# A hybrid decoder step on one core: where norms, decay rows, inverses and loads stand at three borders between stages

## The chip, the core and the metric

The kernel is one program on one core of a Trainium2 chip. The metric is device time in microseconds (us), median over runs; lower is better. TensorE (PE) multiplies matrices, VectorE (DVE), ScalarE (ACT) and GpSimd (POOL) work on tiles, and every transfer is issued by SyncE (SP). Each engine executes its own instructions strictly in the order in which the program wrote them and waits on semaphores for the others.

## The reference, cut to what matters

One inference step of a two-layer decoder: layer 0 mixes tokens with a gated DeltaNet, layer 1 with causal pooling, and each layer ends in a gated ConvFFN. There are 1024 prompt tokens with 16 meta tokens ahead, and 64 sample tokens (8 sequences of 8): 1104 columns, worked on as three chunks of 368. All arithmetic is in 32-bit floats.

```python
h = rmsnorm(x, w)                                    # norm of the layer's input
proj = h @ w_in                                      # q, k, v (8 heads each), z (8), b and a (one narrow item)
qkv = silu(causal_dwconv(conv_state, qkv, conv_w))   # width 4; last 3 columns are an output (gconv)
q, k = l2norm(q) * DK**-0.5, l2norm(k)
g = -exp(A_log) * softplus(a + dt_bias); G = cumsum(g)
decay = exp(G_i - G_j)                               # i >= j
T = inverse(I + strict_lower(beta * (k @ k.T) * decay))   # per chunk of 64
U, W = T @ (v*beta), T @ (k*beta*exp(G)); A = (q @ k.T) * decay
# recurrence over chunks:  v_new = U - W S;  o = (q exp(G)) S + A v_new;  S = S exp(G_end) + k_dec.T v_new
x = x + (rmsnorm(o) * silu(z)) @ w_out
x = x + ConvFFN(rmsnorm(x))                          # up, width-3 conv, gate, down
```

## The kernel before

**Matmuls.** Activations lie transposed, 128 features by columns. A matmul in full precision is made of three with split operands: a tile is rounded into a high part (whi, hhi, ghi: a cast on ACT) and a low part (wlo, hlo, glo: the difference, on POOL or DVE), and PE does hi·hi (line 279), lo·hi (280) and hi·lo (281). A weight tile of 128x512 comes by DMA into wst; `Stream.fetch` issues that load and `Stream.prep` writes the two instructions that split it (lines 162 and 163).

**What sets the order.** Python generators write the program. A generator yields a cost, and a small scheduler (`Slots`: a count of ticks and a heap) resumes it when that many ticks have gone by; the main loop ticks as it writes its matmuls. So the order within each engine's row is fixed when the program is written. `Job` chains a generator behind another; `delayed(n, gen)` starts one n ticks later. In the recurrence `weave` mixes the chain of one head with fillers (the next head's preparation, the output projection wo): each filler is due in proportion between two shares of the chain, such as 0.0 to 0.88.

**Start.** `rstd_steps` squares a chunk on ACT (nsq), adds the squares on DVE (nac, line 307) and sums over features on PE (ss, line 311); `scale_steps` then multiplies by the root (nhf, line 333) and splits (hhi on ACT, hlo on DVE or POOL by `even` and `odd`, lines 336 and 339). Chunk 0's norm is written first. `a_first(c)` writes the first four projection items of chunk c, 96 matmuls, while chunk c+1 is normed; chunk 1's sum is paced by `upto`, chunk 2's by `delayed`.

**Projections.** 33 items, in the order of a table, each 3 chunks of 24 matmuls. `conv_chunk` does the width-4 convolution of a q, k or v item (ACT, line 394, then three steps on DVE, line 402; in the last chunk also raw, tailp and three short steps on line 407). A z item has no convolution, a silu alone. Beside them `rows_steps` makes the decay rows (a scan of g on DVE, then R by subtractions), `k_steps` each head's k·k and the matrix Q, and `inverses` all heads' triangular inverses as one long row of DVE pairs (tb and X, lines 562 and 564). At its end X is stored (xb), copied transposed into Qb (line 597) and stored (xt).

**Recurrence.** `load(h)` issues a head's loads (lG, lq, lk, lE, lv), `load2(h)` those of its inverse (lQ, Tbd and Xbd from xt and xb, l8). `newton(h)` corrects the inverse on PE (nw). `prep(h)` makes qk and its decayed form AT, transposes, and so on; `chain(h)` runs the state through the chunks (pc, op). `nxt(0)`, woven into head 0's chain, writes load(1), the loads of xT (the residual, three times 1472 KB), and the first weights of wo (`wd.fetch`, wst from w_out).

**First ConvFFN.** While the last wo matmuls run, chunks of xT are finished (line 1235) and normed (`norm_steps`), and the up-projection's weights are fetched and split (`wu.prep`, `wu.fetch`).

Of the kernel before, what the change touches and what calls it, by code (L numbers as in the profile page):

```python
# [12 lines left out]
AF = mybir.ActivationFunctionType  # L13
ALU = mybir.AluOpType
# [27 lines left out]
TAIL0 = 1024  # L42
# [171 lines left out]
def build(nc, tc, I, O, stop=None):  # L214
    es = ExitStack()
    V, A, G, T, SY = nc.vector, nc.scalar, nc.gpsimd, nc.tensor, nc.sync
    slots = Slots()
# [40 lines left out]
    def v3(a, t=P):  # L258
        return a.rearrange("p (u t) -> p u t", t=t)
# [57 lines left out]
        out.append(r)  # L317
        yield pace

    def norm_steps(xc, wcol, c, tp, psp, tag, pace=1, pace2=1):  # L320
        out = []
        yield from rstd_steps(xc, tp, psp, tag, out, pace)
        yield from scale_steps(xc, wcol, c, tp, out[0], pace=pace2)

    def scale_steps(xc, wcol, c, tp, r, even=V, odd=G, pace=1):
        s = hcol(c, 0, CH)
# [45 lines left out]
    order = [("ba", 0), ("k", 0), ("k", 1), ("k", 2), ("v", 0), ("v", 1), ("v", 2)]  # L372
    order += [("k", h) for h in range(3, H)]

    order += [(t[0], int(t[1])) for t in "q0 q1 z0 q2 z1 q3 z2 q4 z3 q5 z4 q6 z5 q7 z6 v3 z7 v4 v5 v6 v7".split()]
    base = {"q": 0, "k": 8, "v": 16, "z": 24}
    tid = [32 if kd == "ba" else base[kd] + h for kd, h in order]

# [70 lines left out]
    def rows_steps(lg):  # L449
        a_ = slice(32, 40)  # L450
        R = kp.tile([P, NTP], F32, tag="Q", name="R", bufs=2)
        sm = kp.tile([P, NTP], F32, tag="E", name="sm", bufs=2)
        g = kp.tile([P, NTP], F32, tag="E", name="g", bufs=2)
        t1 = kp.tile([P, NTP], F32, tag="Gb", name="t1", bufs=2)[:, :NT]
        t2 = kp.tile([P, NTP], F32, tag="Bb", name="t2", bufs=2)[:, :NT]
        nA = ab.tile([P, 1], F32, name="nA")
        SY.dma_start(out=sm, in_=I["scanm"])
        G.memset(R, 0.0)
        G.memset(g[a_], 0.0)
        silu(R[0:8, :NT], lg[0:8, :NT], AF.Sigmoid)  # L460
        yield 2
        A.activation(t1[a_], lg[a_, :NT], AF.Abs, bias=cv[a_, C_DTB:C_DTB + 1])
        A.activation(t2[a_], lg[a_, :NT], AF.Relu, bias=cv[a_, C_DTB:C_DTB + 1])
        lnexp()
        A.activation(nA[a_], cv[a_, C_ALOG:C_ALOG + 1], AF.Exp)
        yield 1
        A.activation(t1[a_], t1[a_], AF.Exp, scale=-1.0)
        yield 1
        A.activation(t1[a_], t1[a_], AF.Ln, bias=onec[a_])
        yield 2  # L470
        V.tensor_scalar(nA[a_], nA[a_], -1.0, None, op0=ALU.mult)
        V.tensor_tensor(t1[a_], t1[a_], t2[a_], op=ALU.add)
        V.tensor_scalar(g[a_, :NT], t1[a_], nA[a_], None, op0=ALU.mult)
        V.tensor_tensor_scan(R[a_], sm[a_], g[a_], 0.0, op0=ALU.mult, op1=ALU.add)
        SY.dma_start(out=brow_d, in_=R[0:8])
        SY.dma_start(out=grow_d, in_=R[a_])
        l_ = slice(64, 72)
        Gm = v3(R[a_, 0:TAIL0])
        V.tensor_tensor(v3(R[l_, 0:TAIL0]), Gm[:, :, P - 1:P].to_broadcast([8, 8, P]), Gm, op=ALU.subtract)
        Gp = R[a_, TAIL0:NPR]  # L480
        V.tensor_tensor(R[l_, TAIL0:NPR], Gp[:, N_META - 1:N_META].to_broadcast([8, N_META]),
                        Gp, op=ALU.subtract)
        Gs = v3(R[a_, NPR:NT], LS)
        V.tensor_tensor(v3(R[l_, NPR:NT], LS), Gs[:, :, LS - 1:LS].to_broadcast([8, NSEQ, LS]), Gs,
                        op=ALU.subtract)
        yield 16
# [80 lines left out]
    def inverses(sp):  # L567
        Qb = sp.tile([P, 64, 64], F32, name="Qb")
        Qt = sp.tile([P, 16, 16], F32, name="Qt")
        SY.dma_start(out=Qb, in_=qb_d)  # L570
        X = sp.tile([P, 64, 64], F32, name="X")
        tb = sp.tile([P, 1024], F32, name="tb")
        t8 = sp.tile([NTAIL, H * NTAIL], F32, name="t8")
        Xt = sp.tile([P, 16, 16], F32, name="Xt")
        G.memset(t8, 0.0)
        SY.dma_start(out=x8_d.rearrange("h p t -> p h t"), in_=v3(t8, NTAIL))
        for x, m in ((X, 64), (Xt, 16)):
            G.memset(x, 0.0)
# [12 lines left out]
        for a in range(nt):
            r = slice(16 * a, 16 * a + 16)
            SY.dma_start(out=x8_d[:, r, 16 * a:16 * a + 16], in_=Xt[8 * a:8 * a + 8])
        XT = Qb.rearrange("p b a -> p a b")
        SY.dma_start(out=xb_d, in_=flat(X))
        for r in range(0, 64, 16):
            A.copy(XT[:, r:r + 16, :], X[:, r:r + 16, :])
            yield 1.0
        SY.dma_start(out=xt_d, in_=flat(Qb))
        yield 1.0  # L600
# [72 lines left out]
    with ExitStack() as en:  # L673
# [5 lines left out]
        tp = TP()  # L679
# [51 lines left out]
        def delayed(n, gen):  # L731
            yield n
            yield from gen
# [21 lines left out]
        xload(2, 4)  # L755

        def upto(job, n, then):
            while not job.done:
                yield n
                job.step()  # L760
            yield from then

        third = slots.spawn(delayed(11, rstd(2, 1.4)))
        job = slots.spawn(upto(second, 1.6, scale(1, 0.25)))
        a_first(0)
        job.finish()
        job = slots.spawn(scale(2, 0.25), third)
# [131 lines left out]
    while bg:  # L899
        background(9.0)  # L900
    slots.drain()
    SY.dma_start(out=O["gconv_p"], in_=tailp)
    SY.dma_start(out=O["gconv_s"], in_=tails)
    if stop == "A":
        es_l.close()
        ea.close()
# [280 lines left out]
    r0 = []  # L1187
# [64 lines left out]
    def nxt(h):  # L1252
        if h == 0:
            yield from prep0
            load(1)
            for c in range(NCH):
                SY.dma_start(out=xT[:, :, ck_(c)], in_=I["xT"][c])
            wd.fetch()
            yield from newton(1, pq, "pq")
        if h + 1 < H:  # L1260
            yield from prep(h + 1)
            if h + 2 < H:
                load(h + 2)
            if h:
                while "Q" not in heads[h + 1]:
                    yield 0
                yield from newton(h + 1, pq, "pq")
            if h == 0:
                wd.need(1)
                wd.fetch()  # L1270
            nwj[h + 1] = True
# [4 lines left out]
        flush_pend()  # L1276
    chains = True
    zload(0, range(3))
    load2(1)
    banks = itertools.repeat((pw, "pw"))  # L1280

    def wbank():
# [3 lines left out]
    for h in range(H):  # L1286
        cur = nxt(h)
        if h == H - 1:
            early = later.spawn(early_norm())
        weave(chain(h), 24.0, [(cur, 7.45 if h else 10.35, 0.0, 0.88, True), (wo, 11.0 if h > 1 else 6.0, 0.0 if h > 1 else 0.45, 1.0, False)], flush_pend)  # L1290
    while later.q:
        later.tick()
        flush_pend()
# [28 lines left out]
    def xchunk(c):  # L1322
        return xT[:, :, ck_(c)]
# [303 lines left out]
    banks = itertools.cycle(((pw, "pw"), (pd, "pd")))  # L1627
    for _ in wo:
        slots.tick()
        wu.prep()  # L1630
        wu.fetch()

        while started < len(done):
            if started:
                gen = norm_steps(xchunk(started), C_NF0, started, ft, pd, "pd", 2.5, 2)
            else:
                gen = scale_steps(xchunk(0), C_NF0, 0, ft, r0[0], pace=2)
            jobs.append(slots.spawn(gen, jobs[-1] if jobs else None))
            started += 1
    now, begun = [0], set()  # L1640
# [167 lines left out]
```

## Time and profile before

| | |
|---|---|
| median of 3 runs | 2497.41 us (2495.71 to 2498.42) |
| profiled execution | 2497.63 us |
| its span, first to last instruction | 2495.9 us |
| mean granted TensorE clock | 0.986 |
| busy: PE, DVE, ACT, POOL | 2401.8, 1513.1, 969.5, 861.0 us |
| chain that ended last, share of PE, DVE, ACT, issue | 74%, 12%, 4%, 4% |
| DMA moved | 345.04 MB, mean 138 GB/s |

In rows of instructions the first number is the start in us from the span's beginning, the second the duration (of a merged row with xN: from the first's start to the last's end), then engine, line, operation, out<-in, and in brackets how long the engine stood idle before it and what it waited for. A row of the list of waits gives who waited for whom: us in total, times, longest.

### The profile page before, as it was taken

Reading aid. Unit: us, or ns where it says so; the run is one execution under the profiler, and the core shown is the slowest. Engines: PE = TensorE matmul, PEld = TensorE weight load, DVE = VectorE, ACT = ScalarE, POOL = GpSimd, SP = SyncE. Lnnn points to the kernel's source line nnn. Section 1 sums busy time; section 2 is a strip of 40 time slices with the busy share of each in tenths; the row PEclk is TensorE's granted clock in tenths of the full one; section 3 lists DMA queues with packets and bytes.
Section 4 is the critical chain, followed back from the end, with each engine's and each line's share of the span. In section 5 each row is a group of like instructions: output and inputs, shape, how many; then the busy total and the mean of one; then the engine's idle time right before and its main releaser. Section 6 shows DMA issues by size and latency. Waiting matters only on the chain.

```text
span 2495.9 us, 38634 instructions
## 1 busy us (share of the span) xinstructions
PE 2401.8 (96%) x14393; PEld 2347.4 (94%) x14393; DVE 1513.1 (61%) x3010; ACT 969.5 (39%) x2088; POOL 861.0 (34%) x967
## 2 busy tenths in 40 slices
PE   8999999879999799999999999999999999999997
PEld 6899998879998799999999999999999999999996
DVE  6576799535556745555555545787644555555556
ACT  5677222364553533333333213334323223222334
POOL 3366332133333544554554101211113323332342
PEclk9999999989999899999999999999999999999999
DMA  3366421595641235545444366577763111111112
GB/s 137 118 215 219 162 86 64 181 290 176 197 138 49 73 114 171 170 151 172 160 167 153 130 224 199 190 231 191 218 206 129 43 43 47 47 39 47 43 60 80
DMA packets 198684, 345.04 MB, mean 138 GB/s; under 512 B 55504, under 2 KB 66128, under 8 KB 198112
## 3 DMA queue, kind: packets, MB, share of 16 engines
q1 hardware_dynamic: 198496, 342.56, 41.7%
q8 instruction: 114, 1.87, 0.3%
q14 instruction: 74, 0.61, 0.1%
HBM read 258.88 MB, written 83.61 MB: 137 GB/s over the span
## 4 chain that ended last, share of the span: by engine, by line
PE 74%; DVE 12%; ACT 4%; issue 4%; POOL 2%; DMA 2%; SPq 1%; DVEq 0%; POOLq 0%; ACTq 0%
PE up L281 13%; PE up L279 13%; PE up L280 13%; PE dn L279 6%; PE dn L281 6%; PE dn L280 6%; DVE X L564 2%; DVE tb L562 2%; PE ps L279 2%; DVE acc L402 2%; PE ps L280 2%; PE ps L281 2%; PE pool L1497 1%; PE nw L839 1%; DVE acc L1373 1%
## 5 line engine op out<-in xcount | busy, mean ns | idle before, releaser
L279 PE MATMUL up<-hhi,whi 128*128 128x370 f32 (+2 forms) x2112 | 705.2, 334 | 0.0
L1373 DVE SCALAR_TENSOR_TENSOR acc<-up,cv,acc 128x368 f32<-128x368 f32 (+4 forms) x528 | 303.7, 575 | 657.0 <-ACT acc L1365 408.3
L281 PE MATMUL up<-hhi,wlo 128*128 128x370 f32 (+2 forms) x2112 | 698.9, 331 | 0.0
L280 PE MATMUL up<-hlo,whi 128*128 128x370 f32 (+2 forms) x2112 | 696.9, 330 | 0.2 <-POOL hlo L339 0.2
L163 POOL TENSOR_TENSOR wlo<-wst,whi 128x512 fp32r<-128x512 f32 x286 | 381.3, 1344 | 384.8 <-ACT whi L162 370.0
L1437 DVE TENSOR_TENSOR xT<-xT,dn 128x368 f32<-128x368 f32 (+1 forms) x864 | 408.8, 527 | 2.8 <-PE dn L281 2.7
L280 PEld LDWEIGHTS up<-hlo,whi 128*128 128x128 f32 x2112 | 399.1, 189 | 2.6 <-POOL hlo L339 0.5
L279 PEld LDWEIGHTS up<-hhi,whi 128*128 128x128 f32 x2112 | 397.6, 188 | 2.1 <-issue 0.3
L281 PEld LDWEIGHTS up<-hhi,wlo 128*128 128x128 f32 x2112 | 397.8, 188 | 0.0
L1365 ACT ACTIVATE acc<-up,cv 128x368 f32<-128x368 f32 (+1 forms) x264 | 173.2, 656 | 493.4 <-PE up L281 491.8
L279 PE MATMUL dn<-ghi,whi 128*128 128x368 f32 (+1 forms) x1056 | 349.0, 331 | 4.4 <-DVE xT L1437 2.9
L281 PE MATMUL dn<-ghi,wlo 128*128 128x368 f32 (+1 forms) x1056 | 346.1, 328 | 0.7 <-POOL wlo L163 0.7
L280 PE MATMUL dn<-glo,whi 128*128 128x368 f32 (+1 forms) x1056 | 346.0, 328 | 0.3 <-POOL glo L1411 0.3
L1411 POOL TENSOR_TENSOR glo<-acc,ghi 128x368 fp32r<-128x368 f32 (+1 forms) x132 | 133.2, 1009 | 596.7 <-ACT ghi L1410 572.9
L279 PE MATMUL ps<-hhi,whi 128*128 128x372 f32 (+1 forms) x792 | 269.2, 340 | 16.1 <-DVE acc L402 16.0
L280 PE MATMUL ps<-hlo,whi 128*128 128x372 f32 (+1 forms) x792 | 265.9, 336 | 0.9 <-DVE hlo L726 0.6
L281 PE MATMUL ps<-hhi,wlo 128*128 128x372 f32 (+1 forms) x792 | 265.0, 335 | 0.0
L162 ACT CAST whi<-wst 128x512 fp32r<-128x512 f32 x286 | 172.4, 617 | 89.9 <-PE up L280 43.3
L279 PEld LDWEIGHTS dn<-ghi,whi 128*128 128x128 f32 x1056 | 198.3, 188 | 6.6 <-DVE xT L1437 3.5
L280 PEld LDWEIGHTS dn<-glo,whi 128*128 128x128 f32 x1056 | 198.3, 188 | 1.8 <-POOL glo L1411 0.6
L281 PEld LDWEIGHTS dn<-ghi,wlo 128*128 128x128 f32 x1056 | 198.2, 188 | 1.1 <-POOL wlo L163 1.1
L1410 ACT CAST ghi<-acc 128x368 fp32r<-128x368 f32 (+1 forms) x132 | 65.8, 498 | 272.9 <-DVE acc L1408 272.9
(216 smaller groups left out, 3345.4 us busy)
## 6 DMA issues: line engine op xcount, KB each, us to landing
wst<-i_w_up SPq DMA_DIRECT2D x192, 256.0 KB
whi<-ws SPq DMA_DIRECT2D x128, 256.0 KB
wlo<-ws SPq DMA_DIRECT2D x128, 256.0 KB
wst<-i_w_dn SPq DMA_DIRECT2D x88, 256.0 KB
wst<-i_w_in SPq DMA_DIRECT2D x62, 256.0 KB
whi<-ws_None SPq DMA_DIRECT2D x56, 256.0 KB
wlo<-ws_None SPq DMA_DIRECT2D x56, 256.0 KB
ws<-whi SPq DMA_DIRECT2D x48, 256.0 KB
```

The costliest lines, as they stand in the source:

```text
L162: self.nc.scalar.copy(hi, st)
L163: self.nc.gpsimd.tensor_tensor(lo, st, hi.bitcast(F32), op=ALU.subtract)
L279: T.matmul(ps, hi[:, ws], rhi(k), start=start and j == 0, stop=False)
L280: T.matmul(ps, hi[:, ws], rlo(k), start=False, stop=False)
L281: T.matmul(ps, lo[:, ws], rhi(k), start=False, stop=stop and j == n - 1)
L402: V.scalar_tensor_tensor(acc[:, a:n], ps[:, o + a - d:o + n - d], w[3 - d], acc[:, a:n], op0=ALU.mult, op1=ALU.add)
L562: V.tensor_tensor(t, X[:n, 0:k, j:j + 1].to_broadcast([n, k, w]), Qb[:n, j:j + 1, j + 1:m].to_broadcast([n, k, w]), op=ALU.mult)
L1365: A.activation(acc[:, b:], ps[:, o + b:o + CH], AF.Identity, scale=w[2], bias=col(C_FCB + l * NUP + n))
L1373: V.scalar_tensor_tensor(acc[:, i:m], ps[:, o + i - d:o + m - d], w[2 - d], acc[:, i:m], op0=ALU.mult, op1=ALU.add)
L1410: A.copy(ghi, acc)
L1411: G.tensor_tensor(glo, acc, ghi.bitcast(F32), op=ALU.subtract)
L1437: V.tensor_tensor(xT[:, m, s], xT[:, m, s], ps[:, b:CH], op=ALU.add)
```

## The change

Ten edits:

1. Start: `upto` lets 10 ticks go by and then writes a step of the second norm each 0.5 ticks (before: a step each 1.6 from the start); the third norm starts after 15 ticks, not 11.
2. The table of items: z7 goes from between v3 and v4 to the end.
3. Decay rows: an add goes from DVE to POOL, the scaling by nA to ACT, three subtractions to POOL.
4. Inverses: the transposed copy goes from ACT, 4 of 128x1024, to POOL, 8 of 128x512.
5. gconv's two stores are issued when the last item has its first chunk, not after the last item.
6. `load2(1)` stands right behind the projections, ahead of zload(0).
7. In `nxt(0)`, w_out's first weights are fetched ahead of xT.
8. Head 1's preparation (h == 1 in `weave`) is due from a share of 0.2 of the chain, not 0.0; it makes head 2's.
9. First ConvFFN: weights are split and fetched only when chunk 0 is scaled; chunk 0 is scaled at a pace of 1.5 (2 before).
10. Its chunk 2 is normed at a pace of 3.8 (2.5 before) with all its splits on DVE.

```diff
@@ table of items
-    order += [(t[0], int(t[1])) for t in "q0 q1 z0 q2 z1 q3 z2 q4 z3 q5 z4 q6 z5 q7 z6 v3 z7 v4 v5 v6 v7".split()]
+    order += [(t[0], int(t[1])) for t in "q0 q1 z0 q2 z1 q3 z2 q4 z3 q5 z4 q6 z5 q7 z6 v3 v4 v5 v6 v7 z7".split()]
@@ rows_steps
-        V.tensor_tensor(t1[a_], t1[a_], t2[a_], op=ALU.add)
-        V.tensor_scalar(g[a_, :NT], t1[a_], nA[a_], None, op0=ALU.mult)
+        G.tensor_tensor(t1[a_], t1[a_], t2[a_], op=ALU.add)
+        A.activation(g[a_, :NT], t1[a_], AF.Copy, scale=nA[a_])
...
-        V.tensor_tensor(v3(R[l_, 0:TAIL0]), Gm[:, :, P - 1:P].to_broadcast([8, 8, P]), Gm, op=ALU.subtract)
+        G.tensor_tensor(v3(R[l_, 0:TAIL0]), Gm[:, :, P - 1:P].to_broadcast([8, 8, P]), Gm, op=ALU.subtract)
...
@@ inverses
-        for r in range(0, 64, 16):
-            A.copy(XT[:, r:r + 16, :], X[:, r:r + 16, :])
+        for r in range(0, 64, 8):
+            G.tensor_copy(XT[:, r:r + 8, :], X[:, r:r + 8, :])
@@ start
         def upto(job, n, then):
+            yield n
             while not job.done:
-                yield n
                 job.step()
+                yield 0.5
             yield from then
-        third = slots.spawn(delayed(11, rstd(2, 1.4)))
-        job = slots.spawn(upto(second, 1.6, scale(1, 0.25)))
+        third = slots.spawn(delayed(15, rstd(2, 1.4)))
+        job = slots.spawn(upto(second, 10, scale(1, 0.25)))
@@ projections
             if c == 0 and i > AHEAD:
                 a_done(i - 1)
+                if i == len(order) - 1:
+                    SY.dma_start(out=O["gconv_p"], in_=tailp)
+                    SY.dma_start(out=O["gconv_s"], in_=tails)
...
     slots.drain()
-    SY.dma_start(out=O["gconv_p"], in_=tailp)
-    SY.dma_start(out=O["gconv_s"], in_=tails)
+    load2(1)
@@ nxt(0)
             load(1)
+            wd.fetch()
             for c in range(NCH):
                 SY.dma_start(out=xT[:, :, ck_(c)], in_=I["xT"][c])
-            wd.fetch()
@@ recurrence
     zload(0, range(3))
-    load2(1)
...
-(cur, 7.45 if h else 10.35, 0.0, 0.88, True)
+(cur, 7.45 if h else 10.35, 0.2 if h == 1 else 0.0, 0.88, True)
@@ first ConvFFN
-        wu.prep()
-        wu.fetch()
+        if jobs and jobs[0].done:
+            wu.prep()
+            wu.fetch()
...
-                gen = norm_steps(xchunk(started), C_NF0, started, ft, pd, "pd", 2.5, 2)
+                gen = norm_steps(xchunk(started), C_NF0, started, ft, pd, "pd", 2.5 if started == 1 else 3.8, 2,
+                                 odd=G if started == 1 else V)
             else:
-                gen = scale_steps(xchunk(0), C_NF0, 0, ft, r0[0], pace=2)
+                gen = scale_steps(xchunk(0), C_NF0, 0, ft, r0[0], pace=1.5)
```

Three places of the program show how instructions stand before and after. The first is DVE's row at the start, while items of chunks 0 and 1 are projected; L402 (L403 after) is a convolution step, L307 an add of chunk 2's squares. Before:

```order
L402 SCALAR_TENSOR_TENSOR acc<-ps,cv,acc 128x367
L402 SCALAR_TENSOR_TENSOR acc<-ps,cv,acc 128x366
L402 SCALAR_TENSOR_TENSOR acc<-ps,cv,acc 128x365
L307 TENSOR_TENSOR nac<-nsq 128x736
L402 SCALAR_TENSOR_TENSOR acc<-ps,cv,acc 128x367
L402 SCALAR_TENSOR_TENSOR acc<-ps,cv,acc 128x366
L402 SCALAR_TENSOR_TENSOR acc<-ps,cv,acc 128x365
L307 TENSOR_TENSOR nac<-nac,nsq 128x736
```

After:

```order
L403 SCALAR_TENSOR_TENSOR acc<-ps,cv,acc 128x367
L403 SCALAR_TENSOR_TENSOR acc<-ps,cv,acc 128x366
L403 SCALAR_TENSOR_TENSOR acc<-ps,cv,acc 128x365
L403 SCALAR_TENSOR_TENSOR acc<-ps,cv,acc 128x367
L403 SCALAR_TENSOR_TENSOR acc<-ps,cv,acc 128x366
L403 SCALAR_TENSOR_TENSOR acc<-ps,cv,acc 128x365
L307 TENSOR_TENSOR nac<-nsq 128x736
L307 TENSOR_TENSOR nac<-nac,nsq 128x736 x2
```

Before, an add stands behind each item's three steps; now the adds stand together behind all of them.

The second is SP's row at the end of the projections: stores of the last items (vd, zd), gconv's stores, and the loads of head 1's inverse (lQ, Tbd, Xbd, l) and of z (lz). Before:

```order
L555 DMA vd_97<-out 128x1152
L902 DMA o_gconv_p<-tailp 128x72
L903 DMA o_gconv_s<-tails 128x576
L1041 DMA lz<-zd_98 128x384 x3
L800 DMA lQ<-Qd 128x1024
L804 DMA Tbd<-xt 64x8x64
L804 DMA Xbd<-xb 64x8x64
```

After:

```order
L895 DMA o_gconv_p<-tailp 128x72
L896 DMA o_gconv_s<-tails 128x576
L556 DMA vd_97<-out 128x1152
L556 DMA zd_105<-out 128x1152
L803 DMA lQ<-Qd 128x1024
L807 DMA Tbd<-xt 64x8x64
L807 DMA Xbd<-xb 64x8x64
```

gconv's stores now stand ahead of the stores of v7 and z7, and the inverse's loads directly behind these.

The third is POOL's row at the start of the first ConvFFN: splits of the normed activations (hlo) and of up's weights (wlo). Before:

```order
L1461 MEMSET hist 128x120
L339 TENSOR_TENSOR hlo<-nhf,hhi 128x368
L163 TENSOR_TENSOR wlo<-wst,whi 128x512 x2
L339 TENSOR_TENSOR hlo<-nhf,hhi 128x368
L163 TENSOR_TENSOR wlo<-wst,whi 128x512
L339 TENSOR_TENSOR hlo<-nhf,hhi 128x368
L163 TENSOR_TENSOR wlo<-wst,whi 128x512 x2
L339 TENSOR_TENSOR hlo<-nhf,hhi 128x368
L163 TENSOR_TENSOR wlo<-wst,whi 128x512 x3
```

After:

```order
L1465 MEMSET hist 128x120
L339 TENSOR_TENSOR hlo<-nhf,hhi 128x368 x4
L163 TENSOR_TENSOR wlo<-wst,whi 128x512 x8
L339 TENSOR_TENSOR hlo<-nhf,hhi 128x368 x2
L163 TENSOR_TENSOR wlo<-wst,whi 128x512 x2
```

Chunk 0's four hlo on POOL now come ahead of all eight wlo of the first weights.

More of the change, by code (lines that the diff above doesn't have):

```diff
@@ L318, in rstd_steps, with norm_steps @@
         yield pace
-    def norm_steps(xc, wcol, c, tp, psp, tag, pace=1, pace2=1):
+    def norm_steps(xc, wcol, c, tp, psp, tag, pace=1, pace2=1, odd=G):
         out = []
         yield from rstd_steps(xc, tp, psp, tag, out, pace)
-        yield from scale_steps(xc, wcol, c, tp, out[0], pace=pace2)
+        yield from scale_steps(xc, wcol, c, tp, out[0], odd=odd, pace=pace2)
     def scale_steps(xc, wcol, c, tp, r, even=V, odd=G, pace=1):
@@ L478, in rows_steps @@
         Gm = v3(R[a_, 0:TAIL0])
-        V.tensor_tensor(v3(R[l_, 0:TAIL0]), Gm[:, :, P - 1:P].to_broadcast([8, 8, P]), Gm, op=ALU.subtract)
+        G.tensor_tensor(v3(R[l_, 0:TAIL0]), Gm[:, :, P - 1:P].to_broadcast([8, 8, P]), Gm, op=ALU.subtract)
         Gp = R[a_, TAIL0:NPR]
-        V.tensor_tensor(R[l_, TAIL0:NPR], Gp[:, N_META - 1:N_META].to_broadcast([8, N_META]),
+        G.tensor_tensor(R[l_, TAIL0:NPR], Gp[:, N_META - 1:N_META].to_broadcast([8, N_META]),
                         Gp, op=ALU.subtract)
         Gs = v3(R[a_, NPR:NT], LS)
-        V.tensor_tensor(v3(R[l_, NPR:NT], LS), Gs[:, :, LS - 1:LS].to_broadcast([8, NSEQ, LS]), Gs,
+        G.tensor_tensor(v3(R[l_, NPR:NT], LS), Gs[:, :, LS - 1:LS].to_broadcast([8, NSEQ, LS]), Gs,
                         op=ALU.subtract)
@@ L1289, in build @@
             early = later.spawn(early_norm())
-        weave(chain(h), 24.0, [(cur, 7.45 if h else 10.35, 0.0, 0.88, True), (wo, 11.0 if h > 1 else 6.0, 0.0 if h > 1 else 0.45, 1.0, False)], flush_pend)
+        weave(chain(h), 24.0, [(cur, 7.45 if h else 10.35, 0.2 if h == 1 else 0.0, 0.88, True), (wo, 11.0 if h > 1 else 6.0, 0.0 if h > 1 else 0.45, 1.0, False)], flush_pend)
     while later.q:
```

## The prediction

> **What bounds the kernel now.** I read the page first, then PE's waits, then stretches of the span.
>
> ```profile
> span 2495.9 us, 38634 instructions
> PE 2401.8 (96%) x14393; PEld 2347.4 (94%) x14393; DVE 1513.1 (61%) x3010; ACT 969.5 (39%) x2088; POOL 861.0 (34%) x967
> 900.00:1600.00 700.00, 700.00 (x4121) 695.12 (x4120) 386.17 (x798) 229.89 (x474) 266.02 (x293) 1.00 0.50 168
> PE ss L311 <- DVE nac L307: 17.4, 4, 7.5
> PE ps L279 <- DVE acc L402: 16.0, 8, 4.5
> PE wo L279 <- DVE xT L1235: 7.3, 6, 5.0
> PE pc L1120 <- ACT vn L1116: 4.5, 4, 3.4
> PE kk L541 <- DVE Q L543: 4.1, 1, 4.1
> PE qk L1021 <- DVE AT L1023: 3.4, 1, 3.4
> PE qk L1021 <- issue: 2.8, 1, 2.8
> ```
>
> PE is busy 2401.8 of 2495.9 us: no edit can win more than the 94.1 us of idle time and what the lowered clock costs. The stretch 900 to 1600, deep in the ConvFFNs, shows PE busy all 700 us (the columns after the length are PE, PEld, DVE, ACT, POOL, clock, DMA share, GB/s); the change touches nothing there. Every wait on the list lies before 877 us, at the borders that the change rearranges. The forecast is therefore a list of those waits: which go, and which chain ends last in their place.
>
> A wait costs more than itself. The next rows show the granted clock at 0.50 after one:
>
> ```profile
> 20.90:31.15 10.25, 5.06 (x12) 3.95 (x13) 5.84 (x8) 4.08 (x8) 1.50 (x5) 0.50 0.64 234
> 198.40:201.80 3.40, 1.52 (x10) 1.24 (x9) 3.36 (x11) 1.03 (x2) 0.40 (x1) 1.00 0.93 370
> 201.80:205.20 3.40, 3.40 (x13) 3.40 (x12) 2.85 (x7) 3.00 (x4) 2.03 (x5) 0.50 0.28 103
> 457.80:461.20 3.40, 3.40 (x13) 3.40 (x12) 3.22 (x9) 1.18 (x3) 0.00 (x0) 0.50 0.98 414
> 502.20:509.00 6.80, 6.72 (x29) 6.02 (x30) 1.11 (x3) 4.71 (x17) 2.00 (x2) 0.50 1.03 228
> 536.30:546.60 10.30, 9.74 (x44) 9.43 (x45) 1.90 (x5) 4.01 (x14) 6.48 (x5) 0.50 1.05 380
> 809.70:826.00 16.30, 9.28 (x41) 8.62 (x41) 11.47 (x15) 7.40 (x13) 14.63 (x11) 0.79 0.32 110
> 850.35:857.20 6.85, 4.14 (x9) 3.04 (x10) 3.32 (x5) 5.23 (x9) 2.74 (x2) 0.50 0.12 41
> ```
>
> Lost time there is PE's busy time by one minus the clock: 2.5, 1.7, 1.7, 3.4, 4.9, 1.9 and 2.1 us (second row left out, which is at full clock), 18.2 us together. A stretch of 3.4 us in which PE was busy 1.52 us is followed by a stretch at half clock; I price a new wait of about 2 us or more with 1.7 us on top.
>
> The Trainium skill (TensorE: Matmul & The Clock Gate, HAM oscillation) puts the limit higher: it asks for no PE idle gap above about 3.4 us. This trace has a half-clock stretch behind a gap of 1.88 us (PE ss L440, in the second row), so here it doesn't hold; by it, the small waits that I leave standing below would cost no clock, and the sum would be some 3 us lower.
>
> **The change, border by border.**
>
> *Start (second norm's sum).* The sum of chunk 1's squares (ss, line 311) moves from behind 12 matmuls of chunk 0 to behind 60.
>
> ```profile
> 26.09 2.82 PE L311 MATMUL ss<-nac,ck 128*128 128x368 f32 x4 [7.35 <-DVE nac L307]
> 40.69 1.86 DVE L402 SCALAR_TENSOR_TENSOR acc<-ps,cv,acc 128x367 f32<-128x367 f32 x3 [2.26 <-ACT acc L394]
> 47.69 0.92 DVE L307 TENSOR_TENSOR nac<-nac,nsq 128x736 f32<-128x736 f32 x1
> 48.66 1.50 PE L311 MATMUL ss<-nac,ck 128*128 128x368 f32 x4 [0.53 <-DVE nac L307]
> ```
>
> 48 matmuls at 0.17 us (700 us for 4121 in the stretch 900 to 1600) are 8.2 us and fill the 7.35 us wait; the 2.5 us of clock go too. PE then ends chunk 0 some 9.9 us earlier. But chunk 2's sum still needs nac, at 48.61 (47.69 + 0.92): ahead of that, DVE has the same scalings, nine convolution steps and three adds in both orders, with only the 2.26 us hole before 40.69 to close, and the three adds now stand last. So PE comes early and waits, first for the convolution that frees its banks, then for chunk 2's sum, with a half-clock stretch again. Gain between 9.9 (if DVE's whole row moved forward with PE) and -1.7 (one more half-clock stretch). The row nearest is that DVE is full here, so I take 1.0.
>
> *Decay rows.* The add and the scaling leave DVE for POOL and ACT, the three subtractions go to POOL.
>
> ```profile
> 83.21 1.22 ACT L469 ACTIVATE t<-t,onec 8x1104 f32<-8x1104 f32 x1
> 86.70 1.29 POOL L163 TENSOR_TENSOR wlo<-wst,whi 128x512 fp32r<-128x512 f32 x1
> 90.95 2.55 DVE L474 TENSOR_TENSOR_SCAN R<-sm,g 8x1152 f32<-8x1152 f32 x1
> 95.00 1.67 DVE L402 SCALAR_TENSOR_TENSOR acc<-ps,cv,acc 128x304 f32<-128x304 f32 x3
> 96.82 0.64 PE L279 MATMUL ps<-hhi,whi 128*128 128x368 f32 x1 [4.54 <-DVE acc L402]
> 107.00:132.95 25.95, 25.95 (x162) 25.55 (x160) 18.74 (x41) 24.03 (x40) 12.99 (x11) 1.00 0.46 158
> ```
>
> POOL's add: 1.29 us per 512 elements is 2.8 for 1104; the scale on ACT 1.2 as the row of line 469. From 86.7, between POOL's splits, that gives the scan 90.7 for 90.95: no change. What leaves DVE's path are the subtractions, from the scan's end at 93.50 to 95.00: 1.5 us off the 4.54 us wait, and at best a half-clock stretch of 1.7 more. Late next is POOL (about 2.5 us of subtractions ahead of the copies for line 407) and, to 133, ACT, busy 24.03 of 25.95 us, whose chain ends in the 4.1 us wait for Q. It takes most of this back. Between -3.2 and +1.5 us; I take -0.5.
>
> *Inverses: transposed copy to POOL, z7 last.*
>
> ```profile
> 410.00:448.40 38.40, 35.95 (x212) 35.40 (x211) 36.94 (x50) 8.48 (x20) 11.59 (x12) 1.00 0.17 62
> 448.43 5.63 ACT L597 COPY Qb<-X 128x1024 f32<-128x1024 f32 x3 [9.98 <-DVE X L564]
> 454.46 1.87 DVE L402 SCALAR_TENSOR_TENSOR acc<-ps,cv,acc 128x367 f32<-128x367 f32 x3 [6.06 <-ACT acc L394]
> 456.47 0.41 PE L279 MATMUL ps<-hhi,whi 128*128 128x372 f32 x1 [3.67 <-DVE acc L402]
> 464.60 0.60 SPq L804 DMA_DIRECT2D Tbd<-xt  x1
> ```
>
> ACT's three copies (5.63 us) keep v4's convolution waiting, DVE idles 6.06 us, PE 3.67. With the copies on POOL, 3.67 + 1.7 go. Against that: z7 needs no convolution; with it last, v4's (about 9 x 0.6 and 3 x 0.3 us, 6.3) falls into a stage where DVE is busy 36.94 of 38.40 us, so new waits on line 402 come, up to 6.3 us, and the inverse ends at about 454.8. Eight POOL copies of 128x512 are priced between ACT's speed (5.63 us for three twice as long, 0.94 each) and the split's 1.29 at 86.70: 7.5 to 10.3 us, at 1.0 ending near 463. Between -5.4 and +6; I take -1.5, as DVE's 6 idle us and its 6.3 us of new work about cancel and ACT's wait is gone.
>
> *Projections to recurrence.* gconv's two stores, head 1's inverse loads, w_out's weights before xT, and z7.
>
> ```profile
> 497.11 0.91 PE L1021 MATMUL qk<-lq,lk 128*128 128x128 f32 x6 [2.75 <-issue]
> 501.47 0.21 ACT L991 ACTIVATE eGl<-lG 128x8 f32<-128x8 f32 x1 [1.39 <-DMA o_gconv_p<-tailp]
> 513.30 9.92 SPq L1257 DMA_DIRECT2D xT<-i_xT  x3
> 523.26 4.29 SPq L178 DMA_DIRECT2D wst<-i_w_out  x2
> 498.40:546.00 47.60, 36.26 (x212) 32.76 (x211) 13.66 (x33) 27.32 (x86) 16.27 (x16) 0.79 1.00 342
> ```
>
> Before, the first qk waits 2.75 us for the last v's convolution and silu; z7 has a silu alone, which ACT does in about 0.5: 2.0 gone. The second waits 3.4 for AT, which, like eGl, stood behind the gconv store; stored one chunk earlier, 2.2 gone. The clock there: 3.4. The 3.4 us wait for line 1116's vn is ACT's, behind the cast of w_out weights that land after three xT loads (SP 513.30 to 527.55): with the weights first, 3.4 and 4.9 of clock go. Together 15.9. But DMA is full, share 1.00 over 47.6 us, and the same bytes must pass before head 2's loads, which are issued last. If the heads come 13 us sooner, head 2's preparation asks for them sooner, and even delayed by its 0.2 start it would wait 2 to 5 us; the first fifth of head 1's chain runs unfilled, some 2 us more. I take 15.9 less 7.4: -8.5, between -15.9 and -1 (DMA gives all back but the gconv edit).
>
> *Recurrence to ConvFFN.* Chunk 0's splits come before the weights' splits on POOL; chunk 2's go to DVE; its sum comes 12 items of 3 matmuls later.
>
> ```profile
> 808.69 3.01 POOL L163 TENSOR_TENSOR wlo<-wst,whi 128x512 fp32r<-128x512 f32 x2 [2.56 <-ACT whi L162]
> 811.67 0.95 POOL L339 TENSOR_TENSOR hlo<-nhf,hhi 128x368 fp32r<-128x368 f32 x1
> ```
>
> DVE's scaling waits for POOL's hlo, that for two wlo (3.01 us), and xT's additions, which free PE's banks, stand behind: PE waits 5.0. After, the four hlo come first; about 2.3 of it go. The 7.5 us wait for chunk 2's sum goes whole if nac is ready when PE arrives: the adds no longer interleave with chunk 1's scalings, and PE arrives later by 36 matmuls less 12 that now follow chunk 1's sum. The 2.02 us rest of line 311's 17.4 (17.4 - 7.5 - 7.35 - 0.53) and clock of 1.9 + 2.1 stand too: at most 5.0 + 7.5 + 2.0 + 4.0 = 18.5. Against it: eight wlo in a burst at 1.5 us (12 us) before the first up matmuls, 2 to 3 us late; chunk 2's eight splits at 0.53 us on a DVE with other work, 0 to 2; the rest of the 5.0, 2.7; a half-clock stretch, 1.9. -18.5 + 9 = -9.5, between -16 and -3.
>
> Sum: -1.0 - 0.5 - 1.5 - 8.5 - 9.5 = -21.0. The profiled execution took 2497.63 us (span 2495.9, 1.7 around it), 0.2 above the median of 2497.41. So 2476.6 for it and 2476.4 for a median; I say **2476.5**.
>
> **Rivals.** (1) The start keeps its gain: DVE's row moves forward with PE. For it, the 2.26 us hole and ACT's early squares; against it, the adds now last on a full DVE. 9 us more: 2467.5.
> (2) DMA decides the border to the recurrence: head 2's loads land where they did, head 1's gain waits there. For it, the share of 1.00; against it, the weave's later start. Border worth -1: 2484. With the ConvFFN burst at its worst as well, 2490.
> (3) Slower: head 0's inverse loads come too late. SP is served in order, and Tbd's loads, before at 464.60, now stand behind the copies' store and v6's store; head 0's newton matmuls stand in PE's row between the last projections, and everything behind them waits. v6 ends two items (2 x 72 matmuls x 0.17 = 24.5 us) before the projections' end (497.11 - 2.75 = 494.4), its store goes near 473 with 3 us for convolution and silu, and newton's first matmuls come some 8 us before the end, at 486; with 10 us for the loads' way that leaves 3, and each later us is one us at the end. It decides from 24 us of delay on, when POOL's row holds the copies back for two items and a third's start: 24.5 + 6.3 - 3 - 21 = +7, 2504. Against it: between the eight copies stands only one memset.
> (4) The waits only move: PE's idle time was bound by DVE and ACT chains everywhere, 2495 to 2499.
> (5) The gaps that stay don't lower the clock (the 0.50 rows all follow longer ones but one): 3 us less, 2473.5. That is the result that the skill's rule gives.
>
> **How the numbers follow.** Forecast, 2470 to 2483: 0.55. (1) 0.13, (2) 0.15, (3) 0.04, (4) 0.07, (5) 0.06, already inside the forecast's range. To leave out no more than 2 in 10, the range takes in (2) and most of (1): 2464 to 2491. A run of this kernel can tell about 0.2% (5 us) from no change: faster holds the forecast, (1), (2), (5), 0.89; same is (4), 0.07; slower 0.04.
>
> **What would show it.** Right: PE's waits for line 1116's vn and AT at 3.4 us gone, clock of 1.00 where 536 to 546 stood; no 7.5 us wait for nac at the ConvFFN; the 3.67 us wait behind line 597's copies gone; the 7.35 us one gone but waits for line 402's convolution near 40 and 60 us in its place; chunk 2 of the start beginning within 1 us of before. Wrong: DMA waits (lq, lk, lv, lQ, Tbd) of over 5 us at head 1 or 2, waits for wlo at the first up matmuls, or newton waiting for Tbd before the recurrence.

## The result and the profile after

The changed kernel takes 2485.78 us (median of 6 runs, 2479.45 to 2489.28) against 2497.91 us for the kernel before, run beside it (median of 6). The ratio is 0.9944, 95% interval 0.9933 to 0.9955: 14 us faster by the ratio (11 to 17), 12 by the medians. The forecast was 2476.5, within 2464 to 2491. The direction was right, and so were the two stages that paid; the gain was forecast 7 to 9 us too large.

The page of the changed kernel (its profiled execution took 2486.68 us), the lines for span and busy time:

```profile
span 2484.9 us, 38641 instructions
PE 2400.2 (97%) x14393; PEld 2344.9 (94%) x14393; DVE 1506.9 (61%) x3009; ACT 963.2 (39%) x2085; POOL 870.4 (35%) x975
```

PE's busy time hardly moved (2401.8 to 2400.2), though some stretches at half clock were to go: nearly all that was won is idle time, 94.1 to 84.7 us. Nine rows of PE's list of waits after (in all, times, longest) show what most of it is made of now:

```profile
PE ps L279 <- DVE acc L403: 18.7, 12, 3.7
PE ss L311 <- DVE nac L307: 7.0, 3, 3.9
PE ss L441 <- DVE Q L544: 5.2, 3, 1.8
PE wo L279 <- DVE xT L1240: 5.2, 7, 2.7
PE kk L542 <- DVE Q L544: 4.1, 1, 4.1
PE qk L1026 <- DVE AT L1028: 2.5, 1, 2.5
PE dn L279 <- ACT whi L162: 2.5, 1, 2.5
PE pc L1125 <- ACT vn L1121: 1.8, 4, 0.7
PE dn L281 <- POOL wlo L163: 1.3, 1, 1.3
```

Gone: the 7.35 us of nac at the start, the 3.4 us for vn, the qk wait without a releaser, the 2.2 us for lv. Shorter: nac at the ConvFFN (7.5 to 3.9 us) and xT (5.0 to 2.7). Grown: the wait for convolution (16.0 to 18.7 us, 8 to 12 times), the wait of line 441's sums for Q (3.8 to 5.2), and whi and wlo at the down projection (dn).

The start, PE's rows with a wait, shows the 7.35 us come back in pieces:

```profile
42.27 0.41 PE L279 MATMUL ps<-hhi,whi 128*128 128x372 f32 x1 [2.95 <-DVE acc L403]
45.26 0.41 PE L279 MATMUL ps<-hhi,whi 128*128 128x372 f32 x1 [0.73 <-DVE acc L403]
63.07 0.41 PE L279 MATMUL ps<-hhi,whi 128*128 128x372 f32 x1 [3.38 <-DVE acc L403]
```

The stretches of the changed kernel (columns as before: length, PE, PEld, DVE, ACT, POOL, clock, DMA share, GB/s):

```profile
20.90:31.15 10.25, 10.25 (x60) 9.77 (x59) 6.77 (x10) 5.11 (x10) 1.81 (x6) 1.00 0.63 228
448.40:457.00 8.60, 8.12 (x49) 7.84 (x48) 8.11 (x21) 2.53 (x7) 3.54 (x5) 1.00 0.36 152
497.90:501.30 3.40, 3.40 (x17) 3.14 (x16) 1.11 (x3) 2.03 (x7) 0.42 (x1) 0.50 1.22 231
525.20:538.85 13.65, 13.29 (x61) 12.76 (x61) 4.88 (x13) 3.46 (x11) 5.86 (x5) 0.50 1.05 386
801.70:805.10 3.40, 3.40 (x14) 3.40 (x14) 1.96 (x3) 2.16 (x4) 3.14 (x4) 0.50 0.12 35
835.80:842.60 6.80, 5.06 (x12) 3.94 (x13) 2.35 (x4) 5.42 (x9) 5.17 (x4) 0.50 0.19 61
859.70:863.10 3.40, 3.03 (x10) 3.03 (x11) 3.30 (x6) 0.50 (x1) 0.66 (x2) 0.50 0.22 77
```

The second row is the inverse's end: PE busy 8.12 of 8.60 us where it had been 4.93. The fourth is the surprise: with the vn wait removed, head 0's end still runs at half clock, for 13.65 us (10.30 before), with PE busy 13.29 of them.

### The profile page after: what moved, and what is told of

It is laid out like the page before. It is cut to its first block, busy times and chain, and to the rows that moved or that the text cites. A ratio compares the mean times of both kernels' runs of the same rounds, so it can differ in the third digit from the quotient of the medians.

```text
span 2484.9 us, 38641 instructions
## 1 busy us (share of the span) xinstructions
PE 2400.2 (97%) x14393; PEld 2344.9 (94%) x14393; DVE 1506.9 (61%) x3009; ACT 963.2 (39%) x2085; POOL 870.4 (35%) x975
## 4 chain that ended last, share of the span: by engine, by line
PE 75%; DVE 13%; ACT 4%; issue 3%; POOL 2%; DMA 2%; SPq 0%; DVEq 0%; POOLq 0%; ACTq 0%
PE up L281 13%; PE up L279 13%; PE up L280 13%; PE dn L279 6%; PE dn L281 6%; PE dn L280 6%; DVE tb L563 2%; DVE X L565 2%; DVE acc L403 2%; PE ps L279 2%; PE ps L280 2%; PE ps L281 2%; DVE nhf L333 1%; PE wo L279 1%; PE pool L1501 1%
## 5 line engine op out<-in xcount | busy, mean ns | idle before, releaser
L279 PE MATMUL ps<-hhi,whi 128*128 128x372 f32 (+1 forms) x792 | 268.4, 339 | 18.9 <-DVE acc L403 18.7
L279 PEld LDWEIGHTS ps<-hhi,whi 128*128 128x128 f32 x792 | 151.2, 191 | 23.4 <-issue 12.6
```

The source lines that it names most:

```text
L279: T.matmul(ps, hi[:, ws], rhi(k), start=start and j == 0, stop=False)
```

## The experiments

Times are medians; the ratio is to the kernel before, run beside it. First the four groups alone, each put into the kernel before.

```diff
# start_only: only edit 1 (upto waits 10 ticks, then a step each 0.5; third norm from tick 15)
# rows_only:  only edit 3
# mid_only:   only edits 2, 4, 5, 6, 7, 8 (gconv's early stores need z7 last, so they go together)
# ffn_only:   only edits 9, 10
```

> Before with edit 1 alone (second norm's sum behind 60 matmuls, third norm from tick 15). Theory P (the prediction): ACT and DVE are full there and hand the 7.35 us wait on to waits for convolution (line 402); the stretch up to the projections' fifth item gains 1 us at most: 2496 to 2498. Theory T (the two traces): chunk 2 starts its fifth item 0.1 us later than before (84.02 against 83.88): 2497 to 2499, no measurable change. Rival: DVE's row moves forward with PE and nearly all of 7.35 + 2.5 us is kept: 2488.

> Before with edit 3 alone (add, scaling and three subtractions of the decay rows to POOL and ACT). Theory P: 0.5 us gained, 2497. Theory T: POOL's three subtractions, 1.89 + 0.21 + 0.29 us against DVE's 1.22 + 0.16 + 0.21, and one weight split stand ahead of the raw copy that line 407 needs, so ACT's chain to Q runs 1.6 us later: the kk wait ends 1.6 us later, 2499 to 2500, less if the next wait (Q at about 200 us) swallows it. Rival: the subtractions off DVE shorten the 4.54 us wait and that gain lasts: 2494 to 2496.

> Before with edits 2, 4, 5, 6, 7 and 8 (z7 last, transposed copy on POOL, gconv stores, head 1's inverse loads, w_out first, weave from 0.2). Theory P: -1.5 at the inverses and -8.5 at the border, 2487.5. Theory T, from the stretches between the same matmuls in both traces: from +1.6 at 138 us to -11.6 at 584 us, so -13: 2484 to 2485. Rival: DMA holds head 2 where it was and most is given back: 2494 or above.

> Before with edits 9 and 10 (first ConvFFN's weights after chunk 0 is scaled; chunk 2 at a pace of 3.8 with all splits on DVE). Theory P: -9.5, 2488. Theory T: from the traces the border is worth -3.9 at 860 us and about 1 us more is lost behind it to a stretch at half clock: 2493 to 2495. Rival: the give-back in the ConvFFN (waits at 1713 and 1745 us) comes from this edit too, and nothing is left: 2497.

| kernel | us | ratio, 95% interval |
|---|---|---|
| start_only | 2500.12 | 1.0004, 0.9995 to 1.0013 |
| rows_only | 2501.85 | 1.0005, 0.9996 to 1.0014 |
| mid_only | 2485.27 | 0.9940, 0.9928 to 0.9953 |
| ffn_only | 2493.76 | 0.9980, 0.9971 to 0.9989 |

The first two are no measurable change, mid_only is worth 15 us (12 to 18) and ffn_only 5 (3 to 7). Of mid_only's six edits only 7 and 8 were also run apart (below); how the 15 us divide among the others is open. The changed kernel's gain is mid_only's within the interval, so the sum of the parts (about 18) is not fully there; the intervals are too wide to say more. The traces place the same matmuls at these times:

| us | k·k after its wait | first qk | wo after its wait | dn after its wait | span |
|---|---|---|---|---|---|
| before | 137.07 | 497.11 | 814.71 | 874.22 | 2495.9 |
| start_only | 137.41 | 496.82 | 813.59 | 875.22 | 2500.4 |
| rows_only | 139.74 | 499.70 | 816.58 | 878.28 | 2502.6 |
| mid_only | 137.81 | 489.36 | 801.83 | 861.44 | 2484.4 |
| ffn_only | 136.86 | 493.06 | 808.46 | 865.25 | 2489.3 |
| changed | 138.71 | 492.56 | 801.26 | 858.14 | 2484.9 |

A warning stands in the table. ffn_only changes nothing ahead of 797 us and is 4 us early at the first qk; from dn to the end, which the edits hardly touch, the six take between 1621.7 (before) and 1626.8 us (changed). Differences of 2 to 4 us in one stage of one trace are no evidence here. Part of these 5 us can be seen: a wait of the down projection for xT near 1716 to 1730 us, 1.8 us long before and 3.1 in the changed kernel.

**Decay rows.** In rows_only k·k comes 2.7 us late; 1.2 of it is there when chunk 2's fifth item begins (85.06 us, before 83.88), 1.5 come after that. The changed kernel's rows of POOL and DVE show why:

```profile
86.95 2.56 POOL L473 TENSOR_TENSOR t<-t,t 8x1104 f32<-8x1104 f32 x1
94.36 1.89 POOL L480 TENSOR_TENSOR R<-R 8x1024 f32<-8x1024 f32 x1 [4.86 <-DVE R L475]
96.75 1.27 POOL L163 TENSOR_TENSOR wlo<-wst,whi 128x512 fp32r<-128x512 f32 x1
97.97 0.21 POOL L398 COPY raw<-cst 128x24 f32<-128x24 f32 x1
87.47 2.77 DVE L408 SCALAR_TENSOR_TENSOR acc<-raw,cv,acc 128x64 f32<-128x64 f32 x3
91.73 2.55 DVE L475 TENSOR_TENSOR_SCAN R<-sm,g 8x1152 f32<-8x1152 f32 x1 [1.34 <-ACT g L474]
94.31 1.67 DVE L403 SCALAR_TENSOR_TENSOR acc<-ps,cv,acc 128x304 f32<-128x304 f32 x3
98.21 0.93 DVE L408 SCALAR_TENSOR_TENSOR acc<-raw,cv,acc 128x64 f32<-128x64 f32 x3 [2.22 <-POOL raw L398]
```

The raw copy waits behind the subtractions and a weight split (DVE then waits 2.22 us for it), and the three short steps take 2.77 us beside POOL's add. rows_late tells the two apart:

```diff
         Gm = v3(R[a_, 0:TAIL0])
+        yield 5
         G.tensor_tensor(v3(R[l_, 0:TAIL0]), ...)
 ...
-        yield 16
+        yield 11
```

> Before with edit 3, but POOL's three subtractions written 5 ticks later, behind the weight split and the raw copy that line 407 needs. Theory T: the raw copy's delay is what made edit 3 late; with it gone the kk wait ends earlier than before (137.1 us): 135 to 136.5, and the kernel takes 2496 to 2498 where edit 3 alone took 2500 to 2502. Rival: DVE's work beside POOL's (three short steps took 2.77 us beside POOL's add, 1.38 without it) is what costs: the kk wait ends at 137 to 139 all the same, 2499 to 2501.

Measured 2499.7 us, 1.0004 (0.9994 to 1.0013): the rival. The raw copy is in time, but the subtractions now run beside the same short steps. Rows of rows_late:

```profile
91.99 2.55 DVE L475 TENSOR_TENSOR_SCAN R<-sm,g 8x1152 f32<-8x1152 f32 x1 [1.34 <-ACT g L474]
92.73 2.87 POOL L163 TENSOR_TENSOR wlo<-wst,whi 128x512 fp32r<-128x512 f32 x1 [2.97 <-ACT whi L162]
96.05 1.89 POOL L481 TENSOR_TENSOR R<-R 8x1024 f32<-8x1024 f32 x1
96.16 2.61 DVE L408 SCALAR_TENSOR_TENSOR acc<-raw,cv,acc 128x64 f32<-128x64 f32 x3
```

The short steps take 2.61 us in place of 0.93, so from the fifth item to k·k it takes 54.1 us, against 54.7 with the raw copy's wait and 53.2 before.

**W_out's weights first, and head 1's later start.** Each undone in the changed kernel.

```diff
# no7                                        # no8
-            wd.fetch()                      -  0.2 if h == 1 else 0.0, 0.88, True
             for c in range(NCH): ...xT      +  0.0, 0.88, True
+            wd.fetch()
```

> The changed kernel with edit 7 undone (xT's three loads ahead of w_out's first weights). Theory P: the wait for line 1116's vn (3.4 to 5 us) comes back and with it the half clock that followed it, so 8 us slower than the changed kernel: 2492. Theory T: the wait comes back, 4 us, but the half clock at head 0's end is there with and without it (13.65 us in the changed kernel too, with PE busy 13.29 us), so only the wait is paid: 2488. Rival: DMA is full anyway and head 2's loads only move: no difference, 2484.

> The changed kernel with edit 8 undone (head 1 prepares head 2 from a share of 0.0 of its chain). Theory P: the preparation would ask for head 2's loads too early and wait 2 to 5 us for lq, lk, lv at about 530 us: 2486 to 2488. Theory T: no wait for these loads is left in the changed kernel (lk 0.9 us at 511 only), so the filler has room; the stretch at half clock from 525 to 539 us shrinks if denser work ends it: 2480 to 2484. Rival: no difference, 2484.

no7: 2488.24 us, 0.9960 (0.9947 to 0.9973). The wait is back, and the half clock is as it was but for 1 us (15.31 x 0.5 against 13.29 x 0.5), as the theory from the traces had it. no8: 2488.84 us, 0.9956 (0.9945 to 0.9968): the prediction's theory (a wait for head 2's loads), not the one drawn from the two traces; the loads for head 2 were just in time because of the later start. PE's rows of no7 and no8, and no7's stretch at half clock:

```profile
527.02 0.79 PE L1125 MATMUL pc<-vn,kd 128*128 128x128 f32 x2 [5.18 <-ACT vn L1121]
525.66:542.70 17.04, 15.31 (x67) 14.48 (x68) 4.82 (x14) 5.39 (x16) 7.77 (x6) 0.50 1.02 310
...
534.30 1.62 PE L1026 MATMUL qk<-lq,lk 128*128 128x128 f32 x6 [3.98 <-DMA lk<-kd]
```

Both medians lie 2 to 3 us above the changed kernel's and the intervals overlap with its own; the waits of 5.2 and 4.0 us are plain in the traces.

**Chunk 2 in the first ConvFFN.** Three variations of edit 10 in the changed kernel.

```diff
# pace25                              # oddG                   # ss_late
-  2.5 if started == 1 else 3.8, 2,   -  odd=G if started...   -  2.5 if started == 1 else 3.8, 2,
+  2.5, 2,                            +  odd=G)                +  2.5, 2, hold=None if started == 1 else 15,
#                                        (in rstd_steps)       -  yield 2 * pace
#                                                              +  yield hold or 2 * pace
```

> The changed kernel with chunk 2's norm in the first ConvFFN at a pace of 2.5 as before, its splits still on DVE. Theory P: nac is not ready when PE arrives and the 7.5 us wait is back: 3.6 us slower, 2488. Theory T: with 3.8 the squares and adds stand so far apart that each waits behind a convolution that waits for PE (adds at 830.9, 835.0 and 836.3 us, PE at 833.6); at 2.5 both the adds and the sum come earlier, and the wait ends between 3 and 7.5 us: 2484 to 2488.

> The changed kernel with half of chunk 2's splits back on POOL, the pace still 3.8. Theory P: DVE is not the limit there or costs 0 to 2 us: 2482 to 2484. Theory T: the down projection's waits for whi and wlo at 858 us (2.5 and 1.3 us, against 1.5 and 0.8 before) come from ACT's casts, which stand behind casts that wait for DVE's scaling, with four splits of 0.53 us less on DVE these two shrink by 1 to 2 us: 2482. Rival: POOL's hlo (0.84 us and more each) is behind wlo again and PE waits for it: 2486.

> The changed kernel with chunk 2's norm in the first ConvFFN at a pace of 2.5, but its sum (ss) 15 ticks after the last add instead of 5: the squares and adds early, the sum six matmuls later than in the changed kernel. Theory T: PE's 3.9 us wait is there because the adds are spread, so it falls to under 1 us, and the half clock behind it (6.8 us long) to one window: 2479 to 2481. Rival: the wait moves on to the scaling of chunk 2 and the down projection's weights (2.5 and 1.3 us now): 2483 to 2486.

pace25 2485.92 us, 0.9948 (0.9936 to 0.9960); oddG 2485.42, 0.9941 (0.9928 to 0.9954); ss_late 2481.77, 0.9935 (0.9923 to 0.9947). None is told apart from the changed kernel by time. In pace25 the nac wait is 5.1 us, within the 3 to 7.5 of the theory from the traces. In oddG the wait for whi at dn is 3.8 us, not smaller, so the four splits on DVE were not its cause; the theory from the traces was wrong there. In ss_late chunk 2's nac wait is gone, and the next one has taken its place:

```profile
854.64 0.68 PE L279 MATMUL dn<-ghi,whi 128*128 128x368 f32 x1 [6.81 <-ACT whi L162]
849.90:860.15 10.25, 5.01 (x15) 4.53 (x16) 9.34 (x17) 5.62 (x10) 1.41 (x1) 0.50 0.15 50
```

DVE is busy 9.34 of 10.25 us there. By these rows chunk 2's scaling on DVE, and ACT's casts behind it, bound this border next; no run moved the scaling, so that is argued and not shown. Remove one wait, and PE meets the next one.

**Head 0's end at half clock.** 60 extra matmuls of ones in the tail of head 0:

```diff
+        if h == 0:
+            for _ in range(10):
+                T.matmul(pp[:, :P], ones_r, ones_r, start=True, stop=True)
         for b in range(NU):        # and ahead of lines 1164, 1170 and each of the three 1181 groups
```

> The changed kernel with 60 extra matmuls of 128x128 of ones in six groups of ten in head 0's tail (lines 1159 to 1181); their results are overwritten. At full clock they cost about 60 x 0.055 = 3.3 us. Theory T: the 13.65 us at half clock from 525 to 539 come from thin work (18 matmuls of 8 to 16 columns in 3.8 us, then small ones one behind the other), not from a wait: with the extra work most of the stretch runs at full clock, 4 to 7 us won, 3.3 paid: 2480 to 2484. Theory P: the half clock follows a wait (vn) and nothing there is won: 2488. Rival: the chain's latency, not PE, sets this stretch, and the extra work is hidden: 2484 with the clock unchanged.

2494.44 us, 0.9984 (0.9975 to 0.9992): all three theories wrong, 9 to 10 us slower than the changed kernel. The stretch became longer and PE was busy all of it:

```profile
525.40:556.10 30.70, 30.35 (x141) 29.66 (x141) 7.19 (x20) 5.16 (x17) 6.49 (x5) 0.50 0.67 210
540.22 2.37 PE L1191 MATMUL pS<-ones_r 128*128 128x128 f32 x10
```

Ten extra matmuls take 2.37 us, 0.22 each from start to start. At full clock this kernel's 128x128 matmuls start 0.11 us apart (six qk in 0.83 us at 542.26 us of the changed kernel), so the 0.055 of the expectation was too low as well; and the 18 thin matmuls of line 1159 have 16 or 32 columns by their rows, not 8 to 16. More small matmuls did not end the half clock here, they prolonged it.

**All together.** ss_late without edits 1 and 3:

> The changed kernel without edits 1 and 3, and with chunk 2's sum 15 ticks after its adds at a pace of 2.5. Theory T, by adding what the runs gave: edits 2 and 4 to 8 alone -13 to -15 us, edits 9 and 10 alone -5, the later sum -2 to -3 more, edits 1 and 3 worth 0 to +3 and now left out: 2475 to 2479. Rival: edits 1 and 3 cost nothing that lasts, or the parts don't add up since the clock's stretches fall differently: 2481 to 2484.

2482.67 us, 0.9937 (0.9923 to 0.9951): the rival. It beats neither the changed kernel nor ss_late beyond the intervals, so no cost of edits 1 and 3 shows in company, to within about 3 us; alone, each gains nothing.

## Why the prediction was right, and where it was wrong

*Sum.* -21.0 predicted, -11.0 between the two profiled executions (2497.63 to 2486.68), -14 by the ratio. Two terms carried it, as forecast; one of them was half the size, the other larger than forecast, so the errors of the terms partly cancel, and that is luck. The four groups alone add up to about -18; why the whole gives -14 and not -18 is open, and the intervals allow both. In the two traces the changed kernel is 16.1 us ahead at dn and loses 5.1 of that behind it, where the edits hardly reach.

*Start, -1.0: right.* The 7.35 us came back as 2.95 + 0.73 + 3.38 us of convolution waits; a stretch at half clock (64.40 to 67.81 us) follows the last of them, as forecast, and chunk 2's fifth item begins at 84.02 us for 83.88. The first rival (9 us kept) fell with start_only, 1.0004.

*Decay rows, -0.5, between -3.2 and +1.5: its upper end.* Right that the 4.54 us wait shrinks (3.73 in the changed kernel) and that POOL is late next. The step that failed is "no change" for the scan: it begins at 91.73, for 90.95, since DVE's short steps ahead of it were slowed and it then waits 1.34 us for ACT's scaling. From the fifth item to k·k it takes 53.2 us in all four traces of the table without edit 3 and 54.7 in both with it: +1.5, and no measurable change in time alone.

*Inverses, -1.5.* The 3.67 us wait went; convolution waits of 1.13, 0.98 and 0.47 us came; the eight POOL copies took 1.12 us each (estimate 1.0) and ended at 461.4 (near 463). Group and border were measured together, next.

*Projections to recurrence, -8.5 (with the inverses -10): mid_only -15, 12 to 18.* The forecast was low, by errors that partly offset. The second qk still waits 2.5 us for AT, so only 0.9 of its 2.2 went. "With the weights first, 3.4 and 4.9 of clock go": the wait of 3.4 went (no7 brings back 5.2 us), the 4.9 did not. The changed kernel has the half clock there without that wait, and by the prediction's price it costs 6.6 us (13.29 x 0.5). What stands ahead of it is a stretch in which PE is idle for half of the time with no wait over 0.9 us; its row is the second below. The first is a half-clock stretch of before, behind the 2.2 us wait for lv, that the prediction's list left out:

```profile
522.65:526.06 3.41, 3.14 (x15) 3.17 (x16) 0.82 (x2) 0.89 (x3) 0.00 (x0) 0.50 1.06 390
521.79:525.20 3.41, 1.69 (x10) 1.30 (x10) 0.57 (x2) 3.13 (x9) 2.64 (x3) 1.00 1.06 386
```

With it the clock at this border cost 9.8 us before (half of 6.72, 3.14 and 9.74) and 8.3 after (half of 3.40 and 13.29): 1.5 went where 3.4 and 4.9 were to go. Against these terms, which were too large, stood "2 to 5 us" of DMA waits and "some 2" of an unfilled chain, which were too large as well: lk waits 0.9 us and nothing more, and no wait of the list shows the other. (The two reasons add up to 4 to 7; the 7.4 that was taken off lies above both.) The 2.2 us wait for lv, in no term of the sum, went too. no8 shows that the mechanism is real (3.98 us for lk at a start of 0.0, landed at 534.3) and that edit 8 keeps clear of it: the same qk stands at 537.1 in the changed kernel. The prediction priced the wait as if edit 8 were not enough. Rival 2, DMA, fell with it.

*Recurrence to ConvFFN, -9.5: ffn_only -5, 3 to 7.* This term was forecast at twice its size. From wo to dn (the table) the two traces with these edits take 56.8 and 56.9 us, the four without them 59.5 to 61.7. Of its steps, "about 2.3 of the 5.03 go" is exact (2.75 left). "The 7.5 us wait for chunk 2's sum goes whole if nac is ready when PE arrives" failed: nac was not ready, and 3.9 stayed. The prediction's own count gives nearly that: 36 matmuls less 12 at 0.17 us bring PE 4.1 us later, which leaves 3.4, unless the three adds close up. They did not. DVE's adds before (first three rows) and after stand equally far apart, and PE is ready 3.9 us before the last one ends:

```profile
846.39 0.93 DVE L307 TENSOR_TENSOR nac<-nsq 128x736 f32<-128x736 f32 x1 [2.05 <-ACT nsq L303]
850.48 0.92 DVE L307 TENSOR_TENSOR nac<-nac,nsq 128x736 f32<-128x736 f32 x1
851.84 1.16 DVE L307 TENSOR_TENSOR nac<-nac,nsq 128x736 f32<-128x736 f32 x1 [0.45 <-ACT nsq L303]
830.86 0.93 DVE L307 TENSOR_TENSOR nac<-nsq 128x736 f32<-128x736 f32 x1 [1.35 <-ACT nsq L303]
834.95 0.92 DVE L307 TENSOR_TENSOR nac<-nac,nsq 128x736 f32<-128x736 f32 x1
836.31 1.17 DVE L307 TENSOR_TENSOR nac<-nac,nsq 128x736 f32<-128x736 f32 x1 [0.45 <-ACT nsq L303]
837.54 2.82 PE L311 MATMUL ss<-nac,ck 128*128 128x368 f32 x4 [3.90 <-DVE nac L307]
```

ss_late, in which the sum comes later still, has no such wait. The 2.0 us for chunk 1's sum grew to 2.6. The waits for whi and wlo at dn, 1.5 and 0.7 before, grew to 2.5 and 1.3. And the clock was to cost one stretch of 1.9 us: it cost 1.7 + 2.5 + 1.5 in three, more than the 4.0 of before. In ss_late the 3.9 us moved on to dn, whose wait grew from 2.5 to 6.8 us.

*Other rivals.* Rival 3 (newton late) did not occur: no wait for Tbd or lQ stands in the list. Rival 4 (the waits only move) is what happened at the start and to half of the ConvFFN border, not elsewhere. Rival 5 (gaps that stay don't lower the clock) fell: the stretches at half clock at 497.9 and 801.7 us follow waits of 2.5 and 2.7 us (one of 2.95 us lowered nothing, see the last section). Of the signs of being right, the waits behind line 597's copies and for vn came out as named; three did not: AT still waits 2.5 us, nac 3.9, and the clock at head 0's end is still 0.50. None of the signs of being wrong occurred.

## What to carry to other kernels

A wait at a border between stages is worth what the next chain behind it leaves over: before pricing its removal, follow the engine that feeds the wait (here DVE and ACT) to the next place where PE needs it, as ss_late and the start both show. Ask of every stretch at half clock what work stood in it before putting it down to the wait beside it; the vn wait went and the half clock stayed. Single traces of this kernel differ by 4 us in stages that nothing touches, so a part worth 2 us is settled neither by one trace nor by five runs.

## What was not expected of the hardware

A full PE can stay at half clock. In warm_tail PE was busy 30.35 of 30.70 us with 141 matmuls, nearly all of 128 columns or fewer, and the clock stayed at 0.50 throughout. The Trainium skill (TensorE: Matmul & The Clock Gate, What's actually happening) ties the clock to how busy PE has been, with sustained work of about 3.4 us as the way back to full; eight stretches of 3.4 us in a row, the least busy with 3.06, did not bring it back here, so busy time by the profile's rows is not what the gate measures. A full DMA is not what held it down: DMA stood still in these two stretches of warm_tail.

```profile
545.87:549.28 3.41, 3.41 (x17) 3.41 (x17) 1.03 (x4) 0.20 (x1) 0.90 (x1) 0.50 0.00 0
549.28:552.69 3.41, 3.41 (x18) 3.41 (x17) 0.35 (x1) 0.00 (x0) 0.00 (x0) 0.50 0.00 0
```

Matmuls of 128 columns are not enough to hold it down either: 17 of them filled 497.90 to 501.30 us of the changed kernel at half clock, and the next stretch was at 1.00. After a wait among matmuls of 368 columns (201.80 to 205.20 us before) the half clock also ended after one stretch of 3.4 us. What the gate measures is open; no run varied the width alone.

Nor does a wait of some length, or a stretch with PE busy for half of it, always lower the clock. In the changed kernel the wait of 2.95 us that ends at 42.27 us, in the first row, left it at 1.00, where 1.69 us busy from 521.79 to 525.20 us were followed by 0.50:

```profile
40.51:43.92 3.41, 1.65 (x10) 1.68 (x11) 2.18 (x5) 3.40 (x6) 0.29 (x1) 1.00 0.01 2
43.92:47.33 3.41, 2.68 (x16) 2.30 (x14) 3.17 (x5) 2.44 (x4) 0.00 (x0) 1.00 0.01 2
```

DVE and POOL hold each other up for some forms only. The three steps on line 408, which read raw and acc, took 2.77 us beside POOL's add, 2.61 beside its subtractions and 0.93 when POOL had only short copies; POOL's split took 2.87 us beside DVE's scan in rows_late, 1.27 otherwise. The three steps on line 403, which read ps, took 1.67 us beside POOL's subtraction (94.31 to 95.98), as before. The Trainium skill (SBUF — State Buffer, Who interferes with whom) says that a DVE instruction with two inputs in SBUF contends with a GpSimd instruction that reads SBUF, and that the order of issue decides which of the two is blocked; the rows agree.
